# Conv stage of a decoder trunk: copies issued by ScalarE, taps two products later, last taps in a fixed order

## Chip, cores and metric

The kernel runs on one core of a Trainium2 chip. Its time is the device time in microseconds of one execution; three runs of the kernel before gave 2989.8, 2982.26 and 2988.97, median 2988.97. The engines are named PE (TensorE, matmuls), PEld (its weight loads), DVE (VectorE), ACT (ScalarE), POOL (GpSimd) and SP (SyncE, which only issues transfers here). ACT and POOL can issue transfers too. SBUF is the on-chip memory, PSUM holds matmul results in eight banks.

## What is computed

One inference step of a decoder trunk with four layers, for one prompt of 512 tokens and eight samples of 8 tokens, model width 1024, all in fp32. Layers 0 and 3 mix tokens with a Conformer convolution, layer 1 with sparse attention, layer 2 with pooling; each layer ends with a ConvFFN. Only the Conformer convolution is touched by the change:

```python
CONV_WIDTH = 31
CONV_DIM = D_MODEL          # 1024
...
def layer_norm(x, g, b):
    xf = x.astype(F32)
    mu = jnp.mean(xf, -1, keepdims=True)
    var = jnp.mean(jnp.square(xf - mu), -1, keepdims=True)
    return ((xf - mu) * lax.rsqrt(var + EPS) * g.astype(F32) + b.astype(F32)).astype(x.dtype)
...
def depthwise_causal(xp, w):
    return lax.conv_general_dilated(xp, w[:, None, :].astype(xp.dtype), (1,), 'VALID',
                                    dimension_numbers=('NWC', 'WIO', 'NWC'),
                                    feature_group_count=xp.shape[-1])

def conformer_conv(h, prefix, w_in, w_dw, ln_g, ln_b, w_out):
    a, g = jnp.split(h @ w_in, 2, axis=-1)
    u = a * jax.nn.sigmoid(g)
    up = jnp.concatenate([prefix.astype(u.dtype), u], axis=1)
    y = depthwise_causal(up, w_dw)
    y = jax.nn.silu(layer_norm(y, ln_g, ln_b))
    return y @ w_out, up[:, -(CONV_WIDTH - 1):]
```

Around it stand an RMSNorm with a shift and scale (adaLN) from a conditioning vector, and a gated residual sum.

## The kernel before

**Order of the work.** Each stage is written as a list of tasks with a planned length, dependences and a priority (class `Flow`). A list scheduler plays it through with eight PSUM banks and 18 slots of an SBUF pool and so fixes the order in which each engine's instructions are issued. On the chip each engine keeps that order and waits on semaphores. "DMA" tasks are issues by SP, "XQ" stands for the flight of a transfer and occupies no engine.

**Products.** A large product is split in three: an fp32 weight block (`raw`, 1 MB, loaded by SP at L2513, two buffers) is cut into a high part by ACT (L300, four chunks of 512) and a low part by DVE (L305); PE multiplies high by high, high by low and low by high (L349 to L351, or L357 to L360 for both token halves at once). The next block is requested from SP when the last low chunk of a block is done. A token half is 288 columns, 256 of the prompt and 32 of the samples.

**The Conv stage (`f_conv`, L875) goes over eight tiles of 128 channels.** For tiles 0 and 1 the two input halves a and g come out of `f_consume`, for tiles 2 to 7 from `product`, which is planned as four quarters of 24 matmuls, g first. Then for a tile i:

- ACT takes the sigmoid of g (`sig`, L915), DVE multiplies (`glu`, L919 and L920) into the tile `ub`, whose first 31 columns are zero and whose end holds the samples with their prefix (a load per tile).
- SP writes the last 30 prompt columns to the output (`outs`, L923) and the prompt part of `ub` to a scratch tensor in DRAM (`store`, L926).
- SP reads it back four times over (`shift`, L933, four copies of 270 KB): `xs` holds 32 channels in four versions, each shifted by one more token, so that one matmul with 128 rows does four taps of 32 channels. The outer dimension of the source pattern is 4, then 32 channels, then 540 columns.
- DVE builds the diagonal weights `dg` (`diag`, L938), three buffers.
- PE does the taps (`taps`, L945): eight groups of four taps for each of four channel groups, 32 matmuls of 512 columns into bank `pts`; the profile counts 64 for a tile. ACT takes the result to `y` (`take`, L955).
- The samples' convolution is done apart by POOL and DVE (`prods`, `tree`, L980 to L991).

Taps of tiles 0 to 4 are planned in the loop as soon as their copies may be there. Those of tiles 5 to 7 wait for the last product and are done in halves of 256 columns, first half of 5, 6, 7, then the second half.

**The tail (`f_conv_tail`, L1058)** computes layer norm over the channels: sums over channels by PE (`st` and `sq`, L542, means L534), centring (L1096 and after), squares by ACT, the reciprocal deviation `rvar`, then per tile a multiplication (L1126), Silu (L1128), and the split into high and low parts (L1131, L1133). Then the output product `pd` begins (L349 to L351). Between these, PE computes the adaLN vectors of coming layers: SP loads blocks of 512 KB (`ada`, L391) and PE does four matmuls on each (`adaps`, L421; eight in the profile).

`run` calls `f_conv` for layer 0 and, after layer 2, for layer 3, so the stage runs twice, in 77 to 304 us and 2261 to 2478 us of the profiled execution.

**Completion of transfers.** Each transfer that an engine issues signals one of eight semaphores, used in turn; an issue therefore also waits, where its turn comes round, for an earlier transfer.

Of the kernel before, what the change touches and what calls it, by code (L numbers as in the profile page):

```python
# [22 lines left out]
F32 = mybir.dt.float32  # L23
# [12 lines left out]
HP = 256  # L36
CW = 31

TG = 8
XW = 512 + 4 * TG - 4  # L40

UP = 31 + 512
# [150 lines left out]
class Trunk:  # L193
# [681 lines left out]
    def f_conv(self, fl, l, j, dep, wdep, pdep=None):  # L875
# [25 lines left out]
        def up(i):  # L901
            return U[i][:, 0:UP]
# [19 lines left out]
        def outs(i):  # L922
            nc.sync.dma_start(out=O["uc"][j, :, i], in_=U[i][:, UP - 30:])  # L923

        def store(i):
            nc.sync.dma_start(out=I["ub"][j, i], in_=up(i))  # L926

        def shift(i, p):

            x = X[i, p] = self.slot([128, 2, XW], F32, name="xs")  # L930
            for g in range(2):
                u = I["ub"][j, i, 64 * p + 32 * g:64 * p + 32 * g + 32]
                nc.sync.dma_start(out=x[:, g], in_=bass.AP(tensor=u.tensor, offset=u.offset, ap=[[1, 4], [UP, 32], [1, XW]]))  # L933

# [6 lines left out]
        def taps(o, i, a0, a1, c0, c1):  # L941

            for a in range(a0, a1):
                for g in range(4):
                    nc.tensor.matmul(o[32 * g:32 * g + 32, :c1 - c0], DG[i][:, g * TG + a],  # L945
                                     X[i, g // 2][:, g % 2, 4 * a + c0:4 * a + c1], start=(a == 0), stop=(a == TG - 1),
                                     tile_position=(0, 32 * g))

        def conv(i, c0, c1):
            if c0 == 0:  # L950
                P[i, "t"] = self.bank("pts")
            taps(P[i, "t"][:, c0:c1], i, 0, TG, c0, c1)

# [46 lines left out]
        for i in range(8):  # L1000
# [3 lines left out]
            else:  # L1004
# [8 lines left out]
                val[i] = {h: t for h in range(2)}  # L1013
            tp = fl.add("POOL", 0.25, lambda i=i: pre(i), join_end.get(i - 3), pdep, st=1, prio=pr - 2000)
            gs = []
            for h in range(2):
                x = fl.add("ACT", 0.4, lambda a=(i, h): sig(*a), gend[h], give=1, st=1 - h, prio=pr)
                gs.append(fl.add("DVE", 0.58, lambda a=(i, h): glu(*a), x, val[i][h], tp, give=1, sg=h, prio=pr - 1000))
            t = fl.add("DMA", 0.5, lambda i=i: store(i), gs, prio=pr - 1000)
            kept = [fl.add("DMA", 0.6, lambda i=i: outs(i), gs, prio=pr), t]  # L1020
            t = fl.add("XQ", 2.5, lambda: None, t)
            xs = []
            for p in range(2):
                x = fl.add("DMA", 1.0, lambda a=(i, p): shift(*a), t, st=1, prio=pr - 1000)
                xs.append(fl.add("XQ", 3.5, lambda: None, x))
            kept += xs
            xs.append(fl.add("DVE", 1.15, lambda i=i: diag(i), t_wr, tap_end.get(i - 3), prio=pr - 500))
            if i < 7:
# [14 lines left out]
            fl.add("FREE", 0.0, lambda: None, kept, sg=1)  # L1043
            if i < 5:
                tap_end[i] = fl.add("PE", 7.3, lambda i=i: conv(i, 0, 512), xs, take=1, sg=2, prio=pr + 1)
                join_end[i] = fl.add("ACT", 0.62, lambda i=i: take(i), tap_end[i], give=1, prio=pr + 2)
                y[i].append(join_end[i])
            else:
                late[i] = xs
        for h in range(2):  # L1050
            for i in range(5, 8):
                tap_end[i, h] = fl.add("PE", 3.75, lambda a=(i, HP * h, HP * h + HP): conv(*a), late[i], val[7][1],
                                       tap_end.get((i - 1, h)), tap_end.get((i, 0)) if h else None,
                                       take=0 if h else 1, sg=2 if h else 0, prio=7900 + 10 * h)
        self.w_ahead(fl, val[6][1])
# [1675 lines left out]
```

## Time and profile before

| | us |
|---|---|
| median of three runs | 2988.97 |
| profiled execution, device time | 2984.4 |
| its span | 2982.6 |
| PE busy in it | 2803.2 (94%) |
| DVE / ACT / POOL busy | 1600.6 / 975.2 / 510.9 |
| mean granted clock of TensorE | 0.968 of full speed |
| Conv stage of layer 0, 77.4 to 303.7 | 226.3, PE busy 184.64 |
| Conv stage of layer 3, 2261.0 to 2477.8 | 216.8, PE busy 175.71 |

The profile gives, for one execution, busy times, a timeline of each engine with what ended each wait, the chain of waits that leads to the last instruction, and for any stretch the busy time of each engine with the clock that was granted to TensorE (1.00 is 2.4 GHz) and the share and rate of the 16 DMA engines. Busy time alone says little here: PE is busy 94% of the span, and the rest lies in few places. A line such as `PE L945 ... [4.26 <-DMA xs<-ub]` says that PE stood 4.26 us before that instruction until a transfer into `xs` had landed.

### The profile page before, as it was taken

What the parts mean: (1) busy time and instruction counts of PE and PEld (TensorE: products, weight loads), DVE (VectorE), ACT (ScalarE), POOL (GpSimd) and SP (SyncE); (2) the same over time, 40 slices, a digit from 0 to 9 for tenths busy, and PEclk for the clock granted to TensorE, in tenths of its full rate; (3) what the DMA queues carried; (4) which work ended last, traced back from release to release, by engine and by line L of the source; (5) the groups of instructions that cost most, each with busy time, mean ns of one, the idle gap of its engine ahead of it and who ended that gap; (6) DMA issues with size and microseconds to landing.
All of it is one profiled execution on the core that took longest, in us unless ns stands there. A gap on an engine that the chain in (4) does not pass through costs nothing.

```text
span 2982.6 us, 50711 instructions
## 1 busy us (share of the span) xinstructions
PE 2803.2 (94%) x20677; PEld 2479.5 (83%) x20677; DVE 1600.6 (54%) x3432; ACT 975.2 (33%) x2090; POOL 510.9 (17%) x922
## 2 busy tenths in 40 slices
PE   7798899999989999989999979999998879999998
PEld 5365799999989756889999948999986647999998
DVE  5233664444564676464455596555564435755555
ACT  3012432222354565432222343222232114422223
POOL 3123310000054334110000061000012332200001
PEclk8898999999999999999999989999999989999999
DMA  7426133343344355423322377222232352222221
GB/s 300 139 89 222 58 134 129 141 148 135 141 147 145 118 169 188 156 71 146 110 85 77 102 177 145 85 86 85 86 114 91 112 177 101 73 84 89 82 85 64
DMA packets 105192, 364.42 MB, mean 122 GB/s; under 512 B 27680, under 2 KB 37824, under 8 KB 83712
## 3 DMA queue, kind: packets, MB, share of 16 engines
q1 hardware_dynamic: 102144, 352.79, 36.0%
q0 software_dynamic: 2816, 8.39, 0.8%
q8 instruction: 163, 2.67, 0.4%
q14 instruction: 69, 0.57, 0.1%
HBM read 337.59 MB, written 23.36 MB: 121 GB/s over the span
## 4 chain that ended last, share of the span: by engine, by line
PE 80%; DMA 9%; DVE 6%; issue 1%; SPq 1%; ACT 1%; POOL 1%; DVEq 0%; POOLq 0%; ACTq 0%
PE pa L357 6%; PE pa L360 6%; PE pa L358 6%; PE pb L357 5%; PE pb L358 5%; PE pb L360 5%; PE pd L357 5%; PE pd L358 5%; PE pd L360 5%; DMA xs<-ub 5%; PE pd L349 2%; PE pts L945 2%; PE pd L350 2%; PE pd L351 2%; PE adaps L421 2%
## 5 line engine op out<-in xcount | busy, mean ns | idle before, releaser
L276 DVE TENSOR_TENSOR w<-raw,w 128x2048 fp32r<-128x2048 f32 (+1 forms) x117 | 259.5, 2218 | 386.5 <-ACT w L275 386.5
L357 PE MATMUL pa<-h,w 128*128 128x288 f32 x1280 | 362.7, 298 | 5.6 <-ACT w L275 5.6
L358 PE MATMUL pa<-h,w 128*128 128x288 f32 x1280 | 359.5, 296 | 0.0
L357 PE MATMUL pb<-h,w 128*128 128x288 f32 x1216 | 340.9, 296 | 0.0
L358 PE MATMUL pb<-h,w 128*128 128x288 f32 x1216 | 340.5, 295 | 0.0
L357 PE MATMUL pd<-u,w 128*128 128x288 f32 x1152 | 323.9, 296 | 0.0
L358 PE MATMUL pd<-u,w 128*128 128x288 f32 x1152 | 323.1, 295 | 0.0
L740 POOL COPY so<-ab 128x2 f32<-128x2 f32 x88 | 17.0, 193 | 1516.9 <-ACT ab L710 1516.9
L275 ACT ACTIVATE w<-raw 128x2048 fp32r<-128x2048 f32 (+1 forms) x117 | 218.8, 1870 | 176.3 <-PE pd L360 176.3
L360 PE MATMUL pa<-h,w 128*128 128x288 f32 x1280 | 274.4, 296 | 1.0 <-DVE w L276 1.0
L357 PEld LDWEIGHTS pa<-h,w 128*128 128x128 f32 x1280 | 241.7, 189 | 24.3 <-issue 17.6
L360 PE MATMUL pb<-h,w 128*128 128x288 f32 x1216 | 259.8, 295 | 0.0
L360 PE MATMUL pd<-u,w 128*128 128x288 f32 x1152 | 246.6, 295 | 0.0
L358 PEld LDWEIGHTS pa<-h,w 128*128 128x128 f32 x1280 | 241.9, 189 | 0.0
L945 PE MATMUL pts<-xs,dg 128*32 128x256 f32 (+1 forms) x1408 | 169.8, 553 | 63.5 <-DMA xs<-ub 63.5
L358 PEld LDWEIGHTS pb<-h,w 128*128 128x128 f32 x1216 | 229.0, 188 | 0.0
L357 PEld LDWEIGHTS pb<-h,w 128*128 128x128 f32 x1216 | 228.6, 188 | 0.0
L357 PEld LDWEIGHTS pd<-u,w 128*128 128x128 f32 x1152 | 216.6, 188 | 6.7 <-issue 6.7
L358 PEld LDWEIGHTS pd<-u,w 128*128 128x128 f32 x1152 | 216.8, 188 | 0.0
L305 DVE TENSOR_TENSOR w<-raw,w 128x512 fp32r<-128x512 f32 x201 | 163.2, 853 | 96.2 <-ACT w L300 95.6
L360 PEld LDWEIGHTS pa<-h,w 128*128 128x128 f32 x1280 | 205.8, 189 | 1.5 <-DVE w L276 1.5
L498 DVE TENSOR_TENSOR rtmp<-pd,mod 128x32 f32<-128x32 f32 x368 | 69.0, 187 | 254.7 <-PE pd L360 174.7
(357 smaller groups left out, 6452.4 us busy)
## 6 DMA issues: line engine op xcount, KB each, us to landing
raw<-in_w_dram SPq DMA_DIRECT2D x165, 1024.0 KB
ada<-in_ada_dram SPq DMA_DIRECT2D x192, 512.0 KB
xs<-ub SPq DMA_DIRECT2D x64, 270.0 KB
raw<-in_w_dram SPq DMA_DIRECT2D x16, 768.0 KB
x<-in_x_dram SPq DMA_DIRECT2D x8, 576.0 KB
xsp<-x SPq DMA_DIRECT2D x8, 576.0 KB
x<-xsp SPq DMA_DIRECT2D x8, 576.0 KB
ub<-ub SPq DMA_DIRECT2D x16, 271.5 KB
```

The lines of the kernel that those rows point to most:

```text
L275: nc.scalar.activation(w[:, 0, :width], r[:, :width], AF.Copy)
L276: self.lo_eng.tensor_tensor(w[:, 1, :width], r[:, :width], w[:, 0, :width], OP.subtract)
L305: self.eng(eng).tensor_tensor(w[:, 1, sl], r[:, sl], w[:, 0, sl], OP.subtract)
L349: nc.tensor.matmul(ps[:, :H], hi, mv(k, 0, h), start=first, stop=False)
L350: nc.tensor.matmul(ps[:, :H], hi, mv(k, 1, h), start=False, stop=False)
L351: nc.tensor.matmul(ps[:, :H], lo, mv(k, 0, h), start=False, stop=last)
L357: nc.tensor.matmul(ps[h][:, :H], hi, mv(k, 0, h), start=first, stop=False)
L358: nc.tensor.matmul(ps[h][:, :H], hi, mv(k, 1, h), start=False, stop=False)
L360: nc.tensor.matmul(ps[h][:, :H], lo, mv(k, 0, h), start=False, stop=last)
L421: nc.tensor.matmul(self.a_ps[32 * j:32 * j + 32, 0:N], self.cm[:, k, :], raw[j * N // 1024][:, j * N % 1024:j * N % 1024 + N], start=(k == ...
L498: nc.vector.tensor_tensor(t, self.sv(ps), self.bc(G, m, h), OP.mult)
L945: nc.tensor.matmul(o[32 * g:32 * g + 32, :c1 - c0], DG[i][:, g * TG + a], X[i, g // 2][:, g % 2, 4 * a + c0:4 * a + c1], start=(a == 0), s ...
```

## The change

- The store (L926) and the four copies (L933) of tiles 0 to 6 are issued by ACT instead of SP, and planned as ACT tasks.
- The taps of tile n (0 to 4) are planned with product n+2 and depend on it, so they stand behind it on PE; slots are given back one tile later; `diag` depends on its tile's product.
- Tile 7 has no store: its `xs` is filled by 16 copies of 32 x 540 (69 KB) from `ub` inside SBUF, eight issued by SP and eight by ACT.
- The taps of tiles 5 to 7 stand in one order, (5, first half), (6, first), (5, second), (7, first), (6, second), (7, second), each in two tasks, between which statistics and adaLN matmuls can be placed.

```diff
@@ -923,14 +923,22 @@
             nc.sync.dma_start(out=O["uc"][j, :, i], in_=U[i][:, UP - 30:])
 
         def store(i):
-            nc.sync.dma_start(out=I["ub"][j, i], in_=up(i))
+            nc.scalar.dma_start(out=I["ub"][j, i], in_=up(i))
 
         def shift(i, p):
 
             x = X[i, p] = self.slot([128, 2, XW], F32, name="xs")
             for g in range(2):
                 u = I["ub"][j, i, 64 * p + 32 * g:64 * p + 32 * g + 32]
-                nc.sync.dma_start(out=x[:, g], in_=bass.AP(tensor=u.tensor, offset=u.offset, ap=[[1, 4], [UP, 32], [1, XW]]))
+                nc.scalar.dma_start(out=x[:, g], in_=bass.AP(tensor=u.tensor, offset=u.offset, ap=[[1, 4], [UP, 32], [1, XW]]))
+
+        def shift7(p):
+
+            x = X[7, p] = self.slot([128, 2, XW], F32, name="xs")
+            for g in range(2):
+                for k in range(4):
+                    c = 64 * p + 32 * g
+                    (nc.sync, nc.scalar)[p].dma_start(out=x[32 * k:32 * k + 32, g], in_=U[7][c:c + 32, k:k + XW])
 
         def diag(i):
 
@@ -946,10 +954,10 @@
                                      X[i, g // 2][:, g % 2, 4 * a + c0:4 * a + c1], start=(a == 0), stop=(a == TG - 1),
                                      tile_position=(0, 32 * g))
 
-        def conv(i, c0, c1):
-            if c0 == 0:
+        def conv(i, c0, c1, a0=0, a1=TG):
+            if c0 == a0 == 0:
                 P[i, "t"] = self.bank("pts")
-            taps(P[i, "t"][:, c0:c1], i, 0, TG, c0, c1)
+            taps(P[i, "t"][:, c0:c1], i, a0, a1, c0, c1)
 
         def take(i):
             nc.scalar.activation(yv(i)[:, :, :HP], P[i, "t"].rearrange("p (a c) -> p a c", a=2), AF.Copy)
@@ -1011,20 +1019,27 @@
                     if c:
                         gend = {h: t for h in range(2)}
                 val[i] = {h: t for h in range(2)}
-            tp = fl.add("POOL", 0.25, lambda i=i: pre(i), join_end.get(i - 3), pdep, st=1, prio=pr - 2000)
+            tp = fl.add("POOL", 0.25, lambda i=i: pre(i), join_end.get(i - 4), pdep, st=1, prio=pr - 2000)
             gs = []
             for h in range(2):
                 x = fl.add("ACT", 0.4, lambda a=(i, h): sig(*a), gend[h], give=1, st=1 - h, prio=pr)
                 gs.append(fl.add("DVE", 0.58, lambda a=(i, h): glu(*a), x, val[i][h], tp, give=1, sg=h, prio=pr - 1000))
-            t = fl.add("DMA", 0.5, lambda i=i: store(i), gs, prio=pr - 1000)
-            kept = [fl.add("DMA", 0.6, lambda i=i: outs(i), gs, prio=pr), t]
-            t = fl.add("XQ", 2.5, lambda: None, t)
+            kept = [fl.add("DMA", 0.6, lambda i=i: outs(i), gs, prio=pr)]
             xs = []
-            for p in range(2):
-                x = fl.add("DMA", 1.0, lambda a=(i, p): shift(*a), t, st=1, prio=pr - 1000)
-                xs.append(fl.add("XQ", 3.5, lambda: None, x))
-            kept += xs
-            xs.append(fl.add("DVE", 1.15, lambda i=i: diag(i), t_wr, tap_end.get(i - 3), prio=pr - 500))
+            if i < 7:
+                t = fl.add("ACT", 0.6, lambda i=i: store(i), gs, prio=pr - 1000)
+                kept.append(t)
+                t = fl.add("XQ", 4.0, lambda: None, t)
+                for p in range(2):
+                    x = fl.add("ACT", 1.1, lambda a=(i, p): shift(*a), t, st=1, prio=pr - 1000)
+                    xs.append(fl.add("XQ", 4.0, lambda: None, x))
+            else:
+                for p in range(2):
+                    x = fl.add(("DMA", "ACT")[p], 4.6, lambda p=p: shift7(p), gs, st=1, prio=-1000)
+                    xs.append(fl.add("XQ", 2.0, lambda: None, x))
+                kept += xs
+            xs.append(fl.add("DVE", 1.23, lambda i=i: diag(i), t_wr, tap_end.get(i - 3), [val[i][h] for h in range(2)],
+                             prio=pr - 500))
             if i < 7:
                 t = [fl.add("POOL", 2.7, lambda a=(i, n): prods(*a), gs, st=1, prio=pr + n) for n in range(2)]
                 kept += t
@@ -1041,17 +1056,19 @@
                         t = fl.add("DVE", d, lambda a=(h, n): tree_h(*a), t, sg=1 if n == 1 else 0, prio=-1)
                     y[i].append(t)
             fl.add("FREE", 0.0, lambda: None, kept, sg=1)
-            if i < 5:
-                tap_end[i] = fl.add("PE", 7.3, lambda i=i: conv(i, 0, 512), xs, take=1, sg=2, prio=pr + 1)
-                join_end[i] = fl.add("ACT", 0.62, lambda i=i: take(i), tap_end[i], give=1, prio=pr + 2)
-                y[i].append(join_end[i])
-            else:
-                late[i] = xs
-        for h in range(2):
-            for i in range(5, 8):
-                tap_end[i, h] = fl.add("PE", 3.75, lambda a=(i, HP * h, HP * h + HP): conv(*a), late[i], val[7][1],
-                                       tap_end.get((i - 1, h)), tap_end.get((i, 0)) if h else None,
-                                       take=0 if h else 1, sg=2 if h else 0, prio=7900 + 10 * h)
+            late[i] = xs
+            if i in (2, 3, 4, 5, 6):
+                n = i - 2
+                tap_end[n] = fl.add("PE", 7.3, lambda n=n: conv(n, 0, 512), late[n], [val[i][h] for h in range(2)], take=1,
+                                    sg=2, prio=pr - 900)
+                join_end[n] = fl.add("ACT", 0.62, lambda n=n: take(n), tap_end[n], give=1, prio=pr - 900)
+                y[n].append(join_end[n])
+        t = val[7][1]
+        for i, h in ((5, 0), (6, 0), (5, 1), (7, 0), (6, 1), (7, 1)):
+            for a in range(0, TG, TG // 2):
+                t = fl.add("PE", 1.85, lambda a=(i, HP * h, HP * h + HP, a, a + TG // 2): conv(*a), t, late[i],
+                           take=0 if h or a else 1, sg=2 if h and a else 0, prio=7900)
+            tap_end[i, h] = t
         self.w_ahead(fl, val[6][1])
         self.cv = dict(yv=yv, y=y, bank=lambda i: P[i, "t"], tap_end=tap_end, wdep=val[7][1], gate=[val[n][1] for n in range(8)])
```

Lines of the changed kernel from `store` on carry other numbers: the copies stay L933, tile 7's are L941, `diag` L946, the taps L953, `take` L963, the weight blocks L2530.

How this moves instructions is seen in three places. First ACT, in layer 0, from the sigmoids of tile 1 on (`sg`: sigmoid, `w<-raw`: high parts, `y<-pts`: take-over of taps). Before:

```order
L915 ACTIVATE sg<-pc 128x288 x2
L955 ACTIVATE y<-pts 128x2x256
L300 ACTIVATE w<-raw 128x512
L915 ACTIVATE sg<-pc 128x288
L300 ACTIVATE w<-raw 128x512 x7
L915 ACTIVATE sg<-pc 128x288 x2
L955 ACTIVATE y<-pts 128x2x256 x2
```

And after:

```order
L915 ACTIVATE sg<-pc 128x288 x2
L926 DMA ub<-ub 128x543
L933 DMA xs<-ub 128x1x540 x4
L963 ACTIVATE y<-pts 128x2x256
L300 ACTIVATE w<-raw 128x512
L915 ACTIVATE sg<-pc 128x288
L300 ACTIVATE w<-raw 128x512 x5
L926 DMA ub<-ub 128x543
L300 ACTIVATE w<-raw 128x512 x2
L933 DMA xs<-ub 128x1x540 x4
L915 ACTIVATE sg<-pc 128x288 x4
```

Stores and copies now stand in ACT's order, ahead of take-overs, high parts and sigmoids of later tiles.

Next PE at the last taps of layer 3 (`pts`: taps, `adaps`: adaLN, `st`, `sq`: statistics). Before:

```order
L945 MATMUL pts<-xs,dg 32x256 x32
L421 MATMUL adaps<-ada,cm 32x512 x4
L945 MATMUL pts<-xs,dg 32x256 x64
L421 MATMUL adaps<-ada,cm 32x512 x4
L945 MATMUL pts<-xs,dg 32x256 x64
L421 MATMUL adaps<-ada,cm 32x512 x4
L542 MATMUL st<-y,ones 32x288 x4
L542 MATMUL sq<-sq,ones 32x288 x4
L945 MATMUL pts<-xs,dg 32x256 x32
L534 MATMUL st<-stsb,comb 128x288
L534 MATMUL sq<-stsb,comb 128x288
L542 MATMUL st<-y,ones 32x288 x4
```

And after:

```order
L953 MATMUL pts<-xs,dg 32x256 x32
L421 MATMUL adaps<-ada,cm 32x512 x4
L953 MATMUL pts<-xs,dg 32x256 x64
L421 MATMUL adaps<-ada,cm 32x512 x4
L953 MATMUL pts<-xs,dg 32x256 x16
L421 MATMUL adaps<-ada,cm 32x512 x4
L953 MATMUL pts<-xs,dg 32x256 x16
L421 MATMUL adaps<-ada,cm 32x512 x4
L542 MATMUL st<-y,ones 32x288 x4
L542 MATMUL sq<-sq,ones 32x288 x4
L953 MATMUL pts<-xs,dg 32x256 x16
L534 MATMUL st<-stsb,comb 128x288
```

The means of the first half (L534) now stand ahead of the last 48 matmuls of the taps, before they stood behind all of them.

Last SP at the end of layer 3's stage (`raw`: weight block, `out_uc_dram`: prompt columns to the output, `x<-xsp`: the residual comes back). Before:

```order
L926 DMA ub<-ub 128x543
L923 DMA out_uc_dram<-ub 128x334
L391 DMA ada<-in_ada_dram 128x1024 x2
L2513 DMA raw<-in_w_dram 128x2048
L933 DMA xs<-ub 128x1x540 x4
L391 DMA ada<-in_ada_dram 128x1024 x10
L481 DMA x<-xsp 128x1152 x4
```

And after:

```order
L391 DMA ada<-in_ada_dram 128x1024 x2
L941 DMA xs<-ub 32x540 x8
L2530 DMA raw<-in_w_dram 128x2048
L923 DMA out_uc_dram<-ub 128x334
L391 DMA ada<-in_ada_dram 128x1024 x14
L481 DMA x<-xsp 128x1152 x4
```

The store is gone, half of tile 7's copies stand ahead of the weight block, and fourteen adaLN loads follow where ten did.

## Rows read from the trace of the kernel before

**Rows 1.** The page, costliest groups: line, sizes, count | busy, mean ns | idle before.
```profile
L945 PE MATMUL pts<-xs,dg 128*32 128x256 f32 (+1 forms) x1408 | 169.8, 553 | 63.5 <-DMA xs<-ub 63.5
```

**Rows 2.** Windows: stretch, its us, busy us per engine, PEclk, DMA share, GB/s.
```profile
core 0: us, PE busy (x) PEld busy (x) DVE busy (x) ACT busy (x) POOL busy (x), PEclk, DMA share, GB/s
77.40:94.90 17.50, 12.82 (x66) 2.75 (x65) 0.00 (x0) 0.00 (x0) 0.00 (x0) 0.80 0.11 42
115.60:157.50 41.90, 26.88 (x129) 5.19 (x128) 1.23 (x1) 0.60 (x1) 4.47 (x7) 0.71 0.58 156
157.50:183.20 25.70, 25.70 (x193) 25.53 (x192) 13.99 (x20) 6.42 (x13) 9.71 (x6) 1.00 0.27 96
183.20:200.40 17.20, 12.14 (x65) 2.70 (x64) 0.95 (x1) 0.00 (x0) 5.01 (x7) 0.80 0.52 146
203.70:213.00 9.30, 8.16 (x67) 2.12 (x65) 0.00 (x0) 0.00 (x0) 0.00 (x0) 1.00 0.07 26
249.30:303.70 54.40, 40.70 (x492) 19.37 (x484) 19.57 (x32) 11.90 (x26) 13.54 (x12) 0.84 0.80 249
2277.80:2306.60 28.80, 20.59 (x130) 4.69 (x128) 1.22 (x1) 1.31 (x3) 2.63 (x4) 0.82 0.23 83
2336.10:2351.30 15.20, 11.56 (x66) 2.53 (x64) 0.00 (x0) 0.71 (x2) 2.63 (x5) 0.78 0.39 121
2354.70:2364.90 10.20, 8.51 (x65) 2.22 (x64) 0.00 (x0) 0.00 (x0) 0.00 (x0) 1.00 0.07 27
2383.60:2399.70 16.10, 12.09 (x75) 2.85 (x77) 6.17 (x5) 2.04 (x5) 8.97 (x10) 0.79 0.45 139
2421.50:2477.80 56.30, 36.79 (x482) 20.30 (x480) 19.86 (x33) 11.87 (x25) 13.51 (x12) 0.85 0.80 252
...
2261.00:2477.80 216.80, 175.71 (x1432) 114.41 (x1431) 82.58 (x107) 38.03 (x81) 67.52 (x58) 0.89 0.47 150
```

**Rows 3.** The chain of waits: start us, us, what.
```profile
70.02 15.20 DMA xs<-ub
...
130.99 18.06 DMA xs<-ub
...
205.98 7.05 PE pts L945 x58
...
308.50 0.61 PE pd L350
...
2422.62 15.62 DMA ub<-ub
...
2440.28 18.50 DMA xs<-ub
```

**Rows 4.** Windows over transfers: copies alone, loads alone, two us after a store.
```profile
2284.00:2290.00 6.00, 3.47 (x10) 0.57 (x14) 0.00 (x0) 0.00 (x0) 0.00 (x0) 0.50 0.26 100
2268.00:2274.00 6.00, 6.00 (x36) 6.00 (x35) 5.36 (x7) 0.00 (x0) 2.58 (x2) 0.72 0.96 325
2411.80:2413.80 2.00, 2.00 (x17) 2.00 (x17) 2.00 (x3) 0.00 (x0) 0.77 (x1) 1.00 0.03 8
```

**Rows 5.** Timeline of SP, end of layer 3: start us, us, what is issued.
```profile
2409.83 0.33 SPq L926 DMA_DIRECT2D ub<-ub  x1
...
2414.79 4.27 SPq L933 DMA_DIRECT2D xs<-ub  x4
```

**Rows 6.** Timelines of ACT and DVE in layer 3: the weight split.
```profile
2316.49 2.20 ACT L300 ACTIVATE w<-raw 128x512 fp32r<-128x512 f32 x4 [9.17 <-PE pc L360]
...
2317.30 6.62 DVE L305 TENSOR_TENSOR w<-raw,w 128x512 fp32r<-128x512 f32 x4
```

**Rows 7.** Timeline of PE, end of layer 3; in brackets the wait before.
```profile
2436.36 2.23 PE L421 MATMUL adaps<-ada,cm 128*32 128x512 f32 x6 [11.04 <-DMA ada<-in_ada_dram]
...
2469.66 0.75 PE L534 MATMUL st<-stsb,comb 128*128 128x288 f32 x2
...
2473.96 2.78 PE L421 MATMUL adaps<-ada,cm 128*32 128x512 f32 x24
...
2482.62 0.61 PE L350 MATMUL pd<-h,w 128*128 128x288 f32 x1 [4.32 <-DVE h L1133]
```

## The prediction

> **What bounds the kernel now.** I read the chain of waits first, then windows over the two Conv stages, then the queues. TensorE (PE) carries the kernel, and a depthwise tap matmul is the place where it stands longest for data: 63.5 us of idle time lie before the taps, all of it charged to the transfer that fills xs [rows 1]. The windows put this in time [rows 2]: in most stretches in which taps are due PE is busy for 0.64 to 0.78 of the time and the granted clock falls to 0.71 to 0.85, while in the product stretch 157.50 to 183.20 both are 1.00. The chain names the transfers: at 70.02, 130.99 and 2440.28 PE waits for xs, at 2422.62 for the store ahead of it [rows 3].
>
> Why are these late? The four copies of a tile (270 KB each) take part of the DMA engines only: in 2284 to 2290, with nothing else under way, they moved 100 GB/s at a share of 0.26, so 270/100 = 2.7 us each and 10.9 us a tile; weight and ada loads alone reach 325 GB/s at 0.96 [rows 4]. The store is quick: issued at 2409.83, nothing of it moves after 2411.80 [rows 4, 5]. But SP issues everything in one order: the copies of that tile go out at 2414.79 only, behind a weight block, and SP is held 4.27 us at them [rows 5]. At the end of layer 3, behind ada loads, a store shows as 15.62 and the copies as 18.50 us [rows 3]: some 36 us where 2 + 10.9 would do.
>
> **Work that remains.** One tile's taps need 7.05 us when data is there [rows 3], and eight product quarters took 25.70 us, so 3.21 a quarter and 12.9 a product [rows 2]. These are full-clock prices.
>
> **Part 1, taps of tiles 0 to 4 two products later, copies issued by ScalarE (ACT).** The eight tap stretches [rows 2], less 7.05 a tile:
> - layer 0: 17.50 + 41.90 + 17.20 + 9.30 = 85.9, less 5 x 7.05 = 35.25, leaves 50.7;
> - layer 3: 28.80 + 15.20 + 10.20 + 16.10 = 70.3, less 35.25, leaves 35.0.
>
> That is 85.7 us of waits and lowered clock. No matmul is added. After the change a tile's copies have about two products, 25 us, for what needs 13 to 18 if no SP queue lies ahead. What stays:
> - Tile 0 in layer 0: its taps move by only one quarter of a product (24 matmuls, 3.21) and six other matmuls, from 77.4 to about 81.4; its copies land at 70.02 + 15.20 = 85.2 now. If ACT issues them at once they land about 81 (wait 0); if behind four high-part copies (2.20 us, [rows 6]) about 87 (wait 6). I take 3.
> - Tile 0 in layer 3: seven quarters after 2261.0 instead of four, 2261 + 7 x 3.21 + 2 = 2285.5; its copies now run until about 2288 [rows 4], so 0 to 2.5; I take 1.
> - Statistics of the first half, which lie in the last stretch of layer 3 and stay: 1.
> - Weight low parts: four DVE subtractions took 6.62 us while POOL worked beside them [rows 6]; two chunks, 3.3 us, feed one quarter of 3.21 us, so DVE just keeps up, and about 2 us go where the first is late.
>
> The new wait: an issue on ACT stops ACT until the store has landed and the completion semaphore that is next in turn is free. Queued behind it on ACT are the next product's high parts (2.20 us for four), the sigmoid of the next tile and the take-over of finished taps. DVE's low parts wait for the high parts, PE's product for both, SP's next weight block for the last low part, and a take-over holds a PSUM bank. A high part may come late by a product less its own time and two low chunks, 12.9 - 2.2 - 3.3 = 7.4 us, before PE stands. ACT's work is small: 38.03 us in the 216.80 us of layer 3's stage [rows 2], 4.8 a tile against 27.1. A store's 2 us fit in the 7.4; a store as slow as 15.62 [rows 3] would cost 15.62 - 7.4 = 8 us once. From the bounds 0 and 8 I take 3 for all such places, near the quick store, because SP's bulk loads are no longer issued ahead of it. The issues themselves took SP 4.27 us for four, its standing included [rows 5]; on ACT that lies within its slack. SP, free of them, can send weight blocks earlier, which takes bandwidth from the copies; that is in rival A.
>
> Here the Trainium skill speaks against this part: "DMA: Bandwidth & Descriptors", section "Issuing engines are not separate DMA queues", says that DMAs of the scalar, sync and gpsimd engines run on the same 16 DMA engines and interleave, so a second issuing engine saves only issue time. No row of before shows ACT issuing anything. By the rule the copies would stay nearly as slow as now (rival A); by the rows, where what delays a copy is its place behind blocks of one queue and SP's own standing, most of the delay goes.
>
> **Part 2, the last three tiles.** Now the time from the last products to the steady out-projection is 249.3 to 308.5 = 59.2 us in layer 0 and 2421.5 to 2482.6 = 61.1 in layer 3 [rows 2, 3, 7]. What PE must do in it: taps 3 x 7.05 = 21.2; six ada groups at 2.78/3 = 0.93, about 6; sums and means of the first half, about 2.6. That makes 29.8. The tail of normalisation, from the means' end at 2470.4 to 2482.62, is 12.2 us [rows 7]; the new order puts behind those means the second piece of (6,1), all of (7,1) and two ada groups, 1.8 + 3.5 + 1.9 = 7.2 to 7.4, so 4.8 of the 12.2 stay open: 34.6. Waits for loads come on top: PE waited 11.04 us for one ada load here [rows 7]. In the new SP order fourteen ada loads of 512 KB and one 1 MB block follow, 14 x 1.6 + 3.2 = 25.6 us at 325 GB/s [rows 4], less than the 34.6, so I take 4 out of 0 to 11 a stage. That gives 38.6 against 59.2 and 61.1: 20.6 + 22.5, about 42 us saved after rounding down.
>
> Tile 7's copies no longer pass through DRAM: the store (2 us by [rows 5], 15.62 by [rows 3]) goes, and 16 copies of 69 KB, 1.1 MB, take its place, half on SP, half on ACT: between 3.4 us (325 GB/s) and 11 us (100 GB/s) [rows 4]. They are first needed after (5,0), (6,0) and (5,1), three halves, 10.6 us, and two ada groups after the last product, so the copies are hidden at either end; without that cover they would cost 1 to 7 us. The eight ACT issues stand ahead of nothing PE needs soon but the last high part, whose delay goes on to the raw block and the ada loads behind it; it is in the 4.
>
> Beside this stands the Trainium skill, same page, section "Why a DMA increments its semaphore by 16 and not by 1", which lets the row count of the outer dimension set the number of DMA engines: four for the old pattern, which agrees with the share of 0.26 in [rows 4], sixteen for 32 rows, which no row of before shows. By it the copies end near 3.4 us; the sum doesn't move.
>
> The later dependence of the diagonal weights on the product (DVE, 1.2 us a tile) and a slot given back one tile later cost nothing: DVE has 82.58 busy of 216.80 us [rows 2], and the taps now come two products after.
>
> **Sum.** 85.7 + 42 = 127.7; less 3 + 1 + 1 + 2 + 3 = 10 leaves 118. From the profiled execution, 2984.4 us (4.6 under the median of the runs, 2988.97, which spread over 7.5): **2866 us**. Its own range: with no load wait at the end 8 more are saved, and with the residual 10 gone too it is 2848; with tile 0's waits at 6 and 2.5 and the loads' at 11 twice, 18.5 less, 2885.
>
> **Rivals.**
> A, the copies stay slow. For: same DMA engines, and SP's loads move up. Against: they would no longer queue behind them. A tile has some 25.7 + 7.05 = 33 us from store to taps; at 36 us a tile loses 3 to 5 in some four places (10 to 15), tile 0 of layer 0 loses 6, and tile 1 of layer 0, due about 122.4 in the new order, with copies that landed at 130.99 + 18.06 = 149 now [rows 3], loses up to 27, I take 20. Together about 40 more: 2906.
> B, everything is hidden, at the end too: below 2848.
> C, ACT is held at its issues and the weight split comes late in most tiles: 8 us (a store as slow as 15.62) in ten of the fourteen tiles with a store, 80 of the 118 gone: 2945.
> D, slower: ACT as a serial queue becomes the bound. Store 15.62 and copies 10.9 that ACT must stand for, and 4.8 of its own make 31.3 us a tile, against 27.1 now; beyond 27.1 the stage is longer than before. 4.2 x 14 = +59, of which the last tiles, which need no store for tile 7, give back half their 42: 2984.4 + 59 - 21 = 3022. For: ACT's waits are in program order. Against: quick stores, and ACT needn't stand until the copies land.
> E, no change: the completion turns link ACT's issues to SP's loads, and the old waits come back: 2984.
>
> **How the numbers follow.** Chances: forecast 0.62, A 0.17, B 0.08, C 0.08, D 0.03, E 0.02. The range 2845 to 2912 takes in the forecast's own range, A and most of B; C to E, 0.13, and a tail of B lie outside. A difference of 0.3%, 9 us, is about what can be told from no change here: faster 0.95, within 0.02, slower 0.03.
>
> **What would show it.** In the changed trace: windows over product stretches and taps at a granted clock near 1.00; xs waits under 5 us apart from tile 0 of layer 0; idle time before the taps falling from 63.5 to 5 to 15; from store to last copy under 20 us; the last stretch near 39 us, with its waits on ada loads. Rival A shows as waits on xs with long transfers; C and D as PE waiting for the weights' high and low parts with ACT's queue waiting on the store. I am wrong most easily in the speed of copies beside bulk loads, of which the trace before shows only one queue.

## The result, and the profile after

The changed kernel takes 2875.28 us (median) against 2989.39 before: a ratio of 0.9619, 95% interval [0.9597, 0.9642]. One of its four executions took 3828.29 us at a granted clock of 0.648; the median counts it, the ratio leaves it out, and the median of the other three is 2873.16. The forecast was 2866 with a range of 2845 to 2912. The profiled execution has a span of 2870.7 us, 111.9 less than before, at a granted clock of 0.982 instead of 0.968.

Where it was gained can be read from four stretches, marked by TensorE's own instructions: from the first product matmul of a Conv stage (L357) to its last, and from there to the tenth high-by-high matmul of the output product (L349), that is, to a running output product. All kernels of this study stand in the table (each from its profiled execution; the first instruction of a stretch can lie a few us apart between kernels).

| us | products, layer 0 | end, layer 0 | products, layer 3 | end, layer 3 | ratio to before |
|---|---|---|---|---|---|
| before | 182.5 | 65.9 | 159.7 | 67.0 | 1 |
| **changed kernel** | 143.8 | 43.5 | 134.4 | 46.1 | 0.9619 |
| SP issues again | 140.5 | 58.0 | 117.8 | 49.1 | 0.9610 |
| before, ACT issues | 182.8 | 80.9 | 157.2 | 88.7 | 1.0078 |
| early taps again | 158.7 | 57.3 | 142.1 | 76.3 | 0.9827 |
| tile 7 through DRAM | 144.6 | 61.6 | 136.4 | 58.1 | 0.9711 |
| old last taps | 143.8 | 44.9 | 137.3 | 44.3 | 0.9667 |
| changed, new row order | 125.2 | 43.3 | 115.6 | 46.3 | 0.9492 |
| before, new row order | 132.0 | 46.9 | 124.9 | 46.4 | 0.9584 |
| new row order, no DRAM | 126.3 | 45.3 | 116.2 | 48.7 | 0.9492 |
| new row order, SP issues | 125.2 | 43.5 | 116.1 | 46.0 | 0.9496 |
| new row order, early taps | 130.1 | 49.2 | 116.5 | 59.6 | 0.9573 |

Not all ends hold the same work: 40 to 96 ada matmuls, as the profile counts them, stand in an end (72 and 56 before, 80 and 48 in the changed kernel), and the others stand between the stages or behind them. Eight of them are 0.93 us of work [rows 7]. Differences in time between two kernels are differences of their ratios, times 2989 us.

The change gained 38.7 + 22.4 + 25.3 + 20.9 = 107.3 us there. The group of the taps in the list of groups of after, which answers to [rows 1], lost 42.5 us of busy time (one matmul takes 487 ns on average where it took 553) and 56.3 of idle time:

```profile
L953 PE MATMUL pts<-xs,dg 128*32 128x256 f32 (+1 forms) x1408 | 127.3, 487 | 7.2 <-DMA xs<-ub 5.6 <-DVE y L1099 1.6
```

The windows over the two stages (columns as in [rows 2]: length, busy per engine, granted clock, DMA share, GB/s) show the clock at 0.92 to 1.00, where layer 3's stage before had 0.89 in all and most tap stretches 0.71 to 0.85 [rows 2]:

```profile
62.70:206.50 143.80, 134.13 (x1022) 97.71 (x1021) 57.12 (x70) 26.34 (x56) 60.96 (x51) 0.95 0.54 180
206.50:247.40 40.90, 38.11 (x519) 22.37 (x518) 24.64 (x46) 15.35 (x32) 12.39 (x10) 1.00 0.74 274
2191.90:2326.30 134.40, 120.14 (x946) 88.97 (x945) 52.98 (x69) 26.02 (x56) 56.61 (x52) 0.96 0.47 147
2326.30:2369.80 43.50, 36.83 (x487) 19.50 (x486) 23.86 (x46) 14.88 (x31) 10.96 (x9) 0.92 0.76 284
```

What TensorE still waits for is in its timeline (start, length, instruction, in brackets the wait before and what ended it). First the taps of tile 0 in layer 0, of tiles 0 and 1 in layer 3; then the statistics of the first half in layers 0 and 3; last the end of layer 3:

```profile
82.67 0.76 PE L953 MATMUL pts<-xs,dg 128*32 128x512 f32 x4 [2.26 <-DMA xs<-ub]
...
2217.63 0.64 PE L953 MATMUL pts<-xs,dg 128*32 128x512 f32 x4 [2.13 <-DMA xs<-ub]
...
2233.35 1.07 PE L953 MATMUL pts<-xs,dg 128*32 128x512 f32 x8 [1.17 <-DMA xs<-ub]
...
195.04 1.50 PE L542 MATMUL st<-y,ones 128*32 128x288 f32 x3 [5.12 <-POOL y L1113]
...
2295.03 2.10 PE L542 MATMUL st<-y,ones 128*32 128x288 f32 x10 [10.96 <-ACT y L963]
...
2336.50 3.66 PE L953 MATMUL pts<-xs,dg 128*32 128x256 f32 x64 [1.61 <-DVE y L1099]
2344.09 2.36 PE L421 MATMUL adaps<-ada,cm 128*32 128x512 f32 x6 [3.93 <-DMA ada<-in_ada_dram]
```

The waits for xs are small, as forecast. But the transfers did not become quick. The chain of waits of after shows stores on ACT's queue that take about as long as SP's slow one in [rows 3], 15.62 us:

```profile
2257.33 14.63 DMA ub<-ub
...
2274.90 16.81 DMA ub<-ub
```

And ACT's own timeline around them shows what that does. A store goes out at 2274.90; three high parts later the issue of that tile's copies must wait for the store until 2291.73; behind it stands the take-over of finished taps (L963), for which ACT does nothing for 15.74 us, and for that the statistics of TensorE wait (the row at 2295.03 above):

```profile
2271.99 2.33 ACTq L933 DMA_DIRECT2D xs<-ub  x4
2274.36 0.60 ACT L963 ACTIVATE y<-pts 128x512 f32<-128x512 f32 x1 [15.48 <-DMA xs<-ub]
...
2274.90 2.98 ACTq L926 DMA_DIRECT2D ub<-ub  x1
...
2291.73 2.51 ACTq L933 DMA_DIRECT2D xs<-ub  x4
2294.29 0.60 ACT L963 ACTIVATE y<-pts 128x512 f32<-128x512 f32 x1 [15.74 <-DMA xs<-ub]
```

In layer 0 it is the mean `mu` that ACT computes late behind the same kind of issue, and through it POOL's centring (5.12 us at TensorE):

```profile
194.19 2.36 POOL L1113 TENSOR_TENSOR y<-y,mu 128x288 f32<-128x288 f32 x3 [4.18 <-ACT mu L1159]
```

Why is a store of 271 KB that slow? At 2271.99 to 2274.32 ACT had issued the previous tile's four copies; at 2.7 us each on four engines [rows 4] these alone need 11 us, and the store stands behind them on ACT's own queue. The kernel before had the same on SP's queue. Its chain of waits has two more slow stores besides the one in [rows 3], and each of the three was issued directly behind the four copies of the tile before (here SP's timeline around the second of them):

```profile
177.74 13.45 DMA ub<-ub
...
2328.66 14.04 DMA ub<-ub
```

```profile
2324.37 4.18 SPq L933 DMA_DIRECT2D xs<-ub  x4
2328.66 2.63 SPq L926 DMA_DIRECT2D ub<-ub  x1
```

Now two theories fit the gain. **Lead:** the taps stand two products later, so that 34 us from store to last copy no longer matter, and who issues is of no account. **Queue:** the copies left SP's queue of loads. A third question is whether the form of the copies is the cause of all of it.

### The profile page after: what moved, and what is told of

Its sections match the earlier page's. It is cut to its first block, busy times and chain, and to the rows that moved or that the text cites. A ratio compares the mean times of both kernels' runs of the same rounds, so it can differ in the third digit from the quotient of the medians.

```text
span 2870.7 us, 50713 instructions
## 1 busy us (share of the span) xinstructions
PE 2753.3 (96%) x20677; PEld 2468.7 (86%) x20677; DVE 1589.4 (55%) x3431; ACT 979.4 (34%) x2094; POOL 510.1 (18%) x923
## 4 chain that ended last, share of the span: by engine, by line
PE 51%; DMA 4%; DVE 3%; ACTq 1%; ACT 1%; issue 0%; POOL 0%; SPq 0%; DVEq 0%
PE pa L357 5%; PE pa L360 4%; PE pa L358 4%; PE pb L357 4%; PE pb L360 4%; PE pb L358 4%; PE pd L357 4%; PE pd L360 4%; PE pd L358 4%; PE pd L349 2%; PE pd L350 2%; PE pd L351 2%; DMA ub<-ub 1%; DMA out_ps_dram<-hs 1%; PE pc L350 1%; PE pc L349 1%
## 5 line engine op out<-in xcount | busy, mean ns | idle before, releaser
L357 PE MATMUL pa<-h,w 128*128 128x288 f32 x1280 | 362.3, 298 | 5.6 <-ACT w L275 5.6
L357 PE MATMUL pb<-h,w 128*128 128x288 f32 x1216 | 340.6, 295 | 0.0
L357 PE MATMUL pd<-u,w 128*128 128x288 f32 x1152 | 323.5, 296 | 0.0
L357 PEld LDWEIGHTS pa<-h,w 128*128 128x128 f32 x1280 | 241.6, 189 | 24.3 <-issue 17.6
L357 PEld LDWEIGHTS pb<-h,w 128*128 128x128 f32 x1216 | 228.7, 188 | 0.0
L357 PEld LDWEIGHTS pd<-u,w 128*128 128x128 f32 x1152 | 216.7, 188 | 6.7 <-issue 6.7
L720 ACT ACTIVATE ab<-ab 128x576 f32<-128x576 f32 x88 | 60.4, 687 | 435.9 <-DVE ab L739 435.8
```

What stands on the lines that cost most here:

```text
L357: nc.tensor.matmul(ps[h][:, :H], hi, mv(k, 0, h), start=first, stop=False)
L720: self.nc.scalar.activation(acc, acc, AF.Silu)
```

## Experiments

### SP issues again

```diff
-            nc.scalar.dma_start(out=I["ub"][j, i], in_=up(i))
+            nc.sync.dma_start(out=I["ub"][j, i], in_=up(i))
-                nc.scalar.dma_start(out=x[:, g], in_=bass.AP(...))
+                nc.sync.dma_start(out=x[:, g], in_=bass.AP(...))
-                t = fl.add("ACT", 0.6, lambda i=i: store(i), ...)
+                t = fl.add("DMA", 0.5, lambda i=i: store(i), ...)
-                    x = fl.add("ACT", 1.1, lambda a=(i, p): shift(*a), ...)
+                    x = fl.add("DMA", 1.0, lambda a=(i, p): shift(*a), ...)
```

> The changed kernel, but the store and the four copies of tiles 0 to 6 are issued by SP again; taps two products later, tile 7 and the last taps stay as changed. Theory 'lead': the tap waits went because the taps come two products later; who issues hardly counts, as the copies after ACT's issue still need 16 to 19 us. Then 2860 to 2890, idle time before the taps under 25 us, and the waits of 5.1 and 11.0 us for the statistics (take-overs that stood behind an issue on ACT) gone. Theory 'queue': they went because the copies left SP's queue; then 2915 to 2945, idle before the taps 40 us or more.

Measured: 2875.19 us, ratio 0.9610 [0.9594, 0.9626], the same as the changed kernel. So the issue by ACT brings nothing in sum, and "queue" doesn't explain the gain. The waits for xs before the taps are somewhat longer, 15.3 us:

```profile
L953 PE MATMUL pts<-xs,dg 128*32 128x256 f32 (+1 forms) x1408 | 134.4, 499 | 15.3 <-DMA xs<-ub 15.3
```

and the statistics of layer 3 run without a wait, as the timeline of TensorE shows (no bracket):

```profile
2294.40 1.18 PE L542 MATMUL st<-y,ones 128*32 128x288 f32 x16
```

Two effects nearly cancel: the end of layer 0 is 14.5 us longer, with 6.9 us of waits for xs in it, and the products of layer 3 are 16.6 us shorter (table). Layer 0's tenth output matmul comes 11.3 us later than in the changed kernel (261.3 against 250.0), and from there to layer 3's tenth it takes 10.3 us less (2112.1 against 2122.4).

### The kernel before with ACT's issues alone

The same four lines in the other direction, on the kernel before.

> The kernel before with one edit: store and copies issued by ACT instead of SP, everything else (early taps, old last taps) as before. Theory 'lead': the early taps still find their copies missing; 2960 to 2990, idle before the taps 45 us or more. Theory 'queue': 2905 to 2940, idle before the taps 10 to 25.

Measured: 3015.55 us, ratio 1.0078 [1.0061, 1.0095]: slower by 0.8%, which neither theory had. The products' stretches are about as long as before (182.8 and 157.2 us against 182.5 and 159.7), so an ACT issue doesn't even help early taps; the loss of 15 and 22 us lies in the ends. There the chain of waits has, in layer 3:

```profile
2429.58 24.40 DMA xs<-ub
...
2457.62 29.25 DMA xs<-ub
```

These are the copies of tiles 6 and 7; tile 7's took 18.50 us on SP's queue [rows 3]. There SP issued them at 2438.30, ahead of ten ada loads that follow from 2443.13 on. Here ACT issues tile 7's copies from 2454.73 on, and SP ten ada loads from 2454.94 on, beside them. The records of the single transfers show what that does. On SP's queue tile 7's copies moved 98 GB/s alone, from 2444 to 2446, and 56 to 66 beside the loads behind them, from 2448 to 2456. On ACT's queue they moved 22 to 28 GB/s from 2458 to 2468, while the loads of SP's queue moved 240 to 380. So the two queues share the same engines. The Trainium skill, "DMA: Bandwidth & Descriptors", section "Issuing engines are not separate DMA queues", says that the issuing engine doesn't give a transfer engines of its own; this run and the one above agree.

### Early taps again

```diff
-            if i in (2, 3, 4, 5, 6):
-                n = i - 2
+            if i < 5:
+                n = i
-                tap_end[n] = fl.add("PE", 7.3, ..., late[n], [val[i][h] for h in range(2)], take=1, sg=2, prio=pr - 900)
+                tap_end[n] = fl.add("PE", 7.3, ..., late[n], take=1, sg=2, prio=pr + 1)
```

Not shown are the priority of the take-over and the task `pre`, which go back as well; the planned lengths of the transfers and the later `diag` stay as changed.

> The changed kernel, but taps of tiles 0 to 4 are planned in the loop at once again (as before the change), with ACT's issues, tile 7 and last taps as changed. Theory 'lead': 50 to 80 us slower than the changed kernel, 2925 to 2955. Theory 'queue': within 15 us of it, 2875 to 2890.

Measured: 2942.18 us, ratio 0.9827 [0.9810, 0.9843], so 62 us of the 114 hang on the later place (0.9827 - 0.9619 = 0.0208 of 2989). The waits before the taps are back:

```profile
L953 PE MATMUL pts<-xs,dg 128*32 128x256 f32 (+1 forms) x1408 | 156.0, 524 | 43.3 <-DMA xs<-ub 43.3
```

Of the two theories lead stands and queue falls, but the 62 us are not all waits for copies. Of the 70.9 us between the two profiled executions the table puts 14.9 + 7.7 = 22.6 into the product stretches, where these taps stand, and 13.8 + 30.2 = 44.0 into the ends. In layer 3's end TensorE waits 23.5 us for ada loads, 3.9 in the changed kernel. Over the whole kernel it waits 36.8 us for them, 18.2 in the changed kernel:

```profile
L421 PE MATMUL adaps<-ada,cm 128*32 128x512 f32 (+1 forms) x832 | 121.6, 607 | 36.8 <-DMA ada<-in_ada_dram 36.8
```

72 ada matmuls stand in that end instead of 48, and what follows it is 7.6 us shorter. Nor are the taps quite where they were before the change: in layer 3 those of the five tiles stand behind 103, 103, 295, 319 and 439 product matmuls in the kernel before, 151, 175, 223, 271 and 463 here, and 175, 223, 367, 415 and 511 in the changed kernel. Of the 64.0 us that the change gained in the product stretches, 41.4 are still there in this run; what they come from, no run here tells.

### Another row order in xs

The copies' source has the outer dimension 4 (the shifts). In this kernel the rows of xs, of the stacked weights and of the mask stand in the order channel, shift; the host lays out the weights accordingly, and nothing of the computation changes. Bytes, number of issues and issuers don't change.

```diff
-ap=[[1, 4], [UP, 32], [1, XW]]
+ap=[[UP, 32], [1, 4], [1, XW]]
-    con[:, C_M4:C_M4 + 32] = (p % 32)[:, None] == np.arange(32)[None, :]
+    con[:, C_M4:C_M4 + 32] = (p // 4)[:, None] == np.arange(32)[None, :]
-    A["wst"] = np.ascontiguousarray(wd.transpose(0, 2, 5, 3, 4, 1))...
+    A["wst"] = np.ascontiguousarray(wd.transpose(0, 5, 2, 3, 4, 1))...
-dma_start(out=x[32 * k:32 * k + 32, g], in_=U[7][c:c + 32, k:k + XW])
+dma_start(out=x[k:128:4, g], in_=U[7][c:c + 32, k:k + XW])
```

> The changed kernel with the rows of xs, of the stacked weights and of the mask in another order (channel outside, shift inside), so that the outer dimension of a copy's source is 32 and not 4; same bytes, same number of issues, same issuers. Theory 'pattern': the four engines set a copy's length; the copies of a tile land within 8 us of the first issue instead of 16 to 19, ACT's next store no longer lands behind them, the waits for xs (14.6 us) and most of the 16 us at the statistics go: 2845 to 2862. Rival 'shared': bulk loads beside them set the length; copies still 14 us or more, 2870 to 2880.

Measured: 2840.97 us, ratio 0.9492 [0.9476, 0.9508], better by 38 us than the changed kernel (34 between the two medians) and beyond what I expected. A window over the copies of one tile with no load beside them reads

```profile
2277.00:2280.00 3.00, 3.00 (x36) 0.91 (x32) 3.00 (x2) 0.00 (x0) 3.00 (x2) 1.00 0.89 297
```

a DMA share of 0.89 and 297 GB/s, where the same copies had 0.26 and 100 [rows 4]: 270 KB take some 0.9 us instead of 2.7. It is not the single row that became faster: a row of 2160 bytes takes 103 ns on average in this window and took 90 in the other. More rows move at once, 0.89 x 16 = 14 instead of 0.26 x 16 = 4, and the trace has sixteen records of 4 bytes to a copy here where it had four. This agrees with the Trainium skill's rule, same page, section "Why a DMA increments its semaphore by 16 and not by 1", that the outer dimension sets how many engines a transfer uses. The stores of tiles 2 to 5 of layer 3, 14 to 17 us from issue to last row in the changed kernel, take 2 to 3 here, and taps no longer wait for copies:

```profile
L953 PE MATMUL pts<-xs,dg 128*32 128x256 f32 (+1 forms) x1408 | 121.3, 482 | 1.6 <-DVE y L1099 1.6
```

### The row order alone, on the kernel before

The first three pairs of lines above, in the kernel before.

> The kernel before with one edit: rows of xs in the order channel, shift (outer dimension of the copies' source 32 instead of 4). SP issues, early taps, tile 7 and last taps as before. Theory 'pattern': the copies' slowness made the waits, 63.5 us before the taps fall under 25 and the time to 2915 to 2945. Rival 'place': copies stand behind blocks and loads in SP's queue whatever their own length, and early taps still wait: 2955 to 2985.

Measured: 2862.87 us, ratio 0.9584 [0.9565, 0.9603]. That is as much as the whole change brings (0.9619 [0.9597, 0.9642]), without any of it, and more than "pattern" expected. Idle time before the taps falls from 63.5 to 3.4 us with early taps, copies on SP's queue and the old last taps:

```profile
L945 PE MATMUL pts<-xs,dg 128*32 128x256 f32 (+1 forms) x1408 | 119.2, 477 | 3.4 <-DVE y L1082 2.9 <-DMA xs<-ub 0.4
```

So what [rows 2, 3] show as copies "behind a weight block" was above all the copies' own length: SP's place in the order, which the prediction blamed, stays as it was in this kernel.

### Tile 7 through DRAM again

```diff
-            if i < 7:
+            if i < 8:
                 t = fl.add("ACT", 0.6, lambda i=i: store(i), gs, prio=pr - 1000)
```

> The changed kernel, but tile 7 goes through DRAM like the others (store and four copies, issued by ACT). Theory 'cover short': the in-SBUF copies of the changed kernel have landed 9 us after the last product, ahead of the three halves that hide them; store and copies on ACT's queue need 13 to 19 us and stand behind tile 6's, so PE waits 3 to 10 us a stage at (7, first half): 6 to 22 us slower than the changed kernel. Rival 'hidden anyway': within 5 us of it.

Measured: 2902.61 us, ratio 0.9711 [0.9691, 0.9732], 27 us slower than the changed kernel: the direction of "cover short", but more than its 22. The ends are 18.1 and 12.0 us longer (table). The wait isn't at the taps alone: over the whole kernel, waits of the ada matmuls for loads rise from 18.2 us, the first line below, in the changed kernel, to 30.8, and those of the taps for xs from 5.6 to 13.2:

```profile
L421 PE MATMUL adaps<-ada,cm 128*32 128x512 f32 (+1 forms) x832 | 117.2, 592 | 18.3 <-DMA ada<-in_ada_dram 18.2
...
L421 PE MATMUL adaps<-ada,cm 128*32 128x512 f32 (+1 forms) x832 | 120.8, 602 | 30.8 <-DMA ada<-in_ada_dram 30.8
...
L953 PE MATMUL pts<-xs,dg 128*32 128x256 f32 (+1 forms) x1408 | 128.0, 486 | 15.0 <-DMA xs<-ub 13.2 <-DVE y L1099 1.8
```

### The old order of the last taps

The changed kernel with the `for h`, `for i in range(5, 8)` loop of before in place of the six pairs.

> The changed kernel, but the last taps stand as before: first halves of 5, 6, 7, then second halves, uncut. Theory 'tail covered': taps and ada matmuls no longer lie beside the normalisation's 12.2 us, some 7 us a stage come back, and (7, first half) comes one half earlier: 10 to 20 us slower than the changed kernel. Rival 'loads set the end': the ada loads end the stage either way; within 4 us.

Measured: 2887.63 us, ratio 0.9667 [0.9650, 0.9684], so 14 us slower (0.0048 of 2989), a size that "tail covered" allows. The end of its layer 3 shows the open tail of [rows 7] again: TensorE waits 4.31 us for a low part after the first output matmul.

```profile
2373.44 0.40 PE L349 MATMUL pd<-h,w 128*128 128x288 f32 x1 [1.16 <-ACT h L1147]
2378.15 0.61 PE L350 MATMUL pd<-h,w 128*128 128x288 f32 x1 [4.31 <-DVE h L1149]
```

In the changed kernel the same place of the timeline reads 0.26:

```profile
2365.40 0.40 PE L349 MATMUL pd<-h,w 128*128 128x288 f32 x1 [0.88 <-ACT h L1148]
2366.06 0.40 PE L350 MATMUL pd<-h,w 128*128 128x288 f32 x1 [0.26 <-DVE h L1150]
```

Layer 0 has the same pair, 4.30 against 0.26. So the new order closes the tail. But the ends are no longer without it, 44.9 + 44.3 us against 43.5 + 46.1 (table): they hold 56 and 40 ada matmuls instead of 80 and 48, so what the cover gives is 32 ada matmuls, some 3.7 us of work, done in the same time. Of the 10.8 us between the two profiled executions 2.9 lie in layer 3's products and 9.1 between the stages, where 24 of those matmuls now stand (2.8 us). That the new order is faster is shown; that all 14 us come from the tail is not.

### Three further combinations

Row order as above, and no tile through DRAM: four copies of 270 KB from `ub` to `xs` inside SBUF, two by SP and two by ACT, no store.

> As the run with the other row order, and besides no tile goes through DRAM: four copies of 270 KB from ub inside SBUF, two by SP and two by ACT, no store. Theory: what is left after the row order was ACT standing for stores and a few us at the first tile; 2825 to 2842. Rival: reads inside SBUF or SP's queue make copies as slow as before; 2845 to 2880.

Measured: 2837.85 us, ratio 0.9492 [0.9475, 0.9509], the same as with the store. With short copies the store costs nothing any more.

Row order, with SP as the issuer of tiles 0 to 6:

> The changed kernel with the new row order (channel, shift) and with SP issuing store and copies of tiles 0 to 6. Theory: with the copies short, it makes no difference who issues; within 8 us of the run with the row order and ACT's issues, ratio to the kernel before 0.947 to 0.952. Rival 'SP queue': copies behind weight blocks come late by a block's 3 us each and the ratio is 0.955 or more.

Measured: 2838.39 us, ratio 0.9496 [0.9476, 0.9517]: who issues makes no difference with short copies either.

Row order, with the early taps:

> The changed kernel with the new row order and with the taps of tiles 0 to 4 planned in the loop at once, as before the change. Theory: the two products of lead were needed for the slow copies only; ratio to the kernel before 0.947 to 0.954, idle time before the taps under 8 us. Rival: the lead still covers a store, an issue and a copy, some 5 us at each of ten tiles; ratio 0.960 or more.

Measured: 2862.35 us, ratio 0.9573 [0.9556, 0.9589], between the two expectations, and for another reason than the rival's. The taps wait 0.3 us in all, so the lead has nothing left to cover there. Against the same row order with the lead it loses 5.9 and 13.3 us in the ends of the stages (table). In layer 3's end the ada matmuls wait 14.3 us for their loads, 4.0 with the lead; over the whole kernel it is 30.1 us, 12 more than in the changed kernel. 72 ada matmuls stand in that end instead of 48, and 6.1 of the 13.3 us come back behind it:

```profile
L953 PE MATMUL pts<-xs,dg 128*32 128x256 f32 (+1 forms) x1408 | 126.8, 484 | 0.3 <-DMA xs<-ub 0.3
...
L421 PE MATMUL adaps<-ada,cm 128*32 128x512 f32 (+1 forms) x832 | 122.4, 590 | 30.2 <-DMA ada<-in_ada_dram 30.1
```

Why the loads come later there was not tried. So early taps cost something in the ends that has nothing to do with copies, and part of the 44.0 us in the ends under "Early taps again" may be the same.

## Why the prediction was right, and where its reasons were not

**The time.** 118 us were forecast, 114 came (111.9 in the profiled execution).

**The ends.** Forecast 42 us less; measured 22.4 + 20.9 = 43.3; by the forecast's own measure, from the last product to the first low-part matmul of the output product, 36.5 and 39.1 us against 38.6. One half of the reason is shown: without the in-SBUF copies of tile 7 the ends are 30.1 us longer and the kernel 27 us slower. The other half is not: the new order closes the tail, but the ends are as short without it. And with the new row order alone the ends of the kernel before are 46.9 and 46.4 us, with tile 7 through DRAM and the old last taps. So in the ends, too, most of what part 2 took away was waiting for slow copies, and that the sum of two such reasons came within 2 us is in part luck. The load waits, taken as 4 a stage, are 1.38 and 3.93.

**The first tiles.** Forecast waits of 3 and 1 us; measured 2.26 and 2.13, and 1.17 for the next tile.

**The rest of the tap stretches.** Here 85.7 less the residual 10 gives 75.7 us, and the products' stretches gave 38.7 + 25.3 = 64.0. TensorE stands 24.0 us in them, 9.7 and 14.3, where the residual had 10. The term that was mis-sized is the one for ACT's place, 3 us: it was chosen "near the quick store, because SP's bulk loads are no longer issued ahead of it". The waits behind ACT's issues are 10.96 at the statistics of layer 3, 5.12 at those of layer 0, and 2.29 at a product of layer 0 that waited for a late sigmoid, 18.4 in all. The bound of a store "as slow as 15.62" was the right row; the stores took 14.63 and 16.81. The prediction read that row as a store "behind ada loads". In the trace of before the three slow stores of the chain stand directly behind the copies of the tile before, and the quick one of [rows 4, 5] has none ahead. So what makes a store slow went over to ACT's queue with the copies. That the two runs in which ACT doesn't issue slow copies (SP issues; other row order) lack these waits shows the cause. The 2 us for late low parts were not needed: TensorE waits for none there.

**The reason behind part 1** was half wrong. It gave the gain to the copies leaving SP's queue and to the lead together, and expected store to last copy under 20 us. The store at 2257.33 alone took 14.63, and the copies issued behind it at 2271.99 held up the next store until 2291.71: 34 us. So rival A's premise, slow copies, held, and with it the Trainium skill's rule on issuing engines; only its price of 40 us was wrong, since the lead covers 34 us nearly everywhere: the waits for xs at the taps of the first five tiles are 5.56 us in all. Two runs decide it: ACT's issue undone costs nothing (0.9610 against 0.9619), done alone it makes the kernel before slower (1.0078). The lead is the part that holds, with the limits given under "Early taps again".

**The rivals C and D** describe what is seen on ACT, though not at the weight split: the take-over and the mean stood behind the issue, not the high parts. ACT's serial queue came near the bound: from the store at 2257.33 to the next at 2274.90 it stood for the store, issued four copies and took over finished taps, 14.66 + 2.37 + 0.54 = 17.6 us, and TensorE's own work is 12.9 + 7.05 = 20 us a tile.

**What lay underneath.** The prediction read from [rows 4] that the copies use a quarter of the DMA engines, computed their 10.9 us a tile from it, and then looked only at where they stand in a queue. The row order alone brings 0.9584. The change worked around slow copies; making them short is worth as much (0.9619), and both together give 0.949 to 0.950, some 37 us better than the changed kernel. Among those three kernels the intervals tell no difference. One row was read loosely: the window of [rows 4] that the prediction calls loads alone, 325 GB/s, has a store and 149 KB of copies in it besides; the sum uses it only to hold 25.6 us of loads against 34.6.

## What to carry to other kernels

When a transfer's window shows a DMA share far under what loads reach, ask first for its form: the order of its dimensions can be worth more than any place in a queue. Moving an issue to a compute engine puts that engine's next instructions behind the transfer that the issue waits for, so look at who is queued there, and count slow transfers of the same queue ahead of it. Lead, a consumer placed later, hides slow transfers without making them faster; here it held each buffer for one tile longer.

## What was not expected of the hardware

- The same 270 KB copy, with the same rows of 2160 bytes, ran at 100 GB/s with 4 outside and at 297 GB/s with 32 outside, alone in both cases.
- Tile 7's copies, issued by ACT beside ada loads from SP, took 29.25 us in the chain of waits; on SP's queue, with the loads issued behind them, 18.50. A separate queue made them slower, not faster.
- A store of 271 KB took 2 us with nothing ahead of it on its queue, and 13.45 to 16.81 us directly behind four slow copies, on SP's queue as on ACT's.
